# Two token mixers: how the decay sums and the adaLN rows are computed

## The chip, the cores and the metric

The kernel runs on one core of a Trainium2 chip. What counts is the device time of one execution in microseconds; less is better. A core has five engines with one instruction queue each: TensorE (PE in the profile, its weight loads PEld), VectorE (DVE), ScalarE (ACT), GpSimd (POOL) and SyncE (SP), which here issues the loads from memory. The engines meet only at semaphores.

## The reference

A trunk of two layers. Each layer is a feed-forward part, a token mixer and a second feed-forward part, each with its own modulation by a vector `c`. All sizes: 256 tokens, width 1024, float32 in and out.

```python
mod = (silu(c) @ w_ada[layer] + b_ada[layer]).reshape(b, 3, 3, 1, 1024)   # shift, scale, gate of each part
u = modulate(x, mod[:, 1, 0], mod[:, 1, 1])
m = hybrid_mixer(u, ...)                            # the token mixer
x = layer_norm(alpha * x + (1 + mod[:, 1, 2]) * m, ...)
u = modulate(x, mod[:, 2, 0], mod[:, 2, 1])         # second feed-forward part
# inside the mixer, scan over chunks with H = 8 heads:
a = dt * A
a_cs = cumsum(a)
decay = exp(where(causal, a_cs[l] - a_cs[s], -inf))
y_diag = einsum(C, B, decay, x * dt)
```

`mod` is nine rows of 1024 values per layer: one row vector times a 1024 x 1024 matrix for each. `decay` is, for each head, a 128 x 128 matrix for each of the two blocks of 128 tokens.

## The kernel before

The 256 tokens stand in two tiles of 128 (`t` = 0, 1). Every weight is streamed from memory once, as half tiles of 128 x 1024 float32 (512 KB, names `raw_...`). A pool has nine buffers for them (`NRAW`), and SyncE issues the loads in the order of use, up to nine ahead (`AHEAD`, `issue_loads`); a load into a buffer waits for the last reader of the tile that was in it. An ordinary weight is split: ScalarE casts it to a high part in fp32r (`h...`), VectorE subtracts to get the low part (`l...`). Each product of the large matrices is three fp32r matmuls (`mm3`): high by high, low by high, high by low.

The weights of `mod` are treated otherwise. Each of the nine rows of a layer (`ch` = 0 to 8) is a stream of eight half tiles `raw_(layer, ch, q)_h`. In `ada_step` VectorE multiplies a half tile by its 128 values of silu(c) and adds it to an accumulator `ada` of 128 x 1024. After the eighth, `ada_post` sums the 128 partitions by four float32 products with ones (`pr`, 32 equal rows for each 256 columns). A shift or scale row is copied by ScalarE (`adc`), turned into columns by TensorE (`pm`) and the bias is added. A gate row is split into `adg` (ScalarE's high part, VectorE's low part), spread over 128 partitions by fp32r products (`pg`) and VectorE writes `gate`; its bias is loaded into a row of the accumulator at the start.

Mixer 0 streams 16 such half tiles (its own gate, `ch` 5, then row 7, the scale of the part that follows); mixer 1 streams eight (its own gate). In both they stand between the input weights (`z`) and the output weights `w2`, `w3`, `w0`, `w1` of the mixer, two half tiles each.

Inside a mixer the order in which work is handed out is a string table `MIX` (`st` is one half tile of the stream, `am` `seg_pre`, `seg` the decay sums, `v` and `z` input products with names `ovx` and `ozx`, `y` `pdx`, `tf` `pyx`, which turns the result `yc` so that its features lie on the partitions, `p` the output projection `accx`). The order in which TensorE then runs its matmuls is fixed when the program is built: a scheduler takes from what the table handed out what its own estimate holds ready. Each engine runs its queue in that order.

The decay sums: `seg_pre` makes for each head `am`, the mask `gtm` scaled by that head's column of `a` (ScalarE, 128 x 128, eight for each `t`). `seg` multiplies each by the mask `tri` in one float32 product of 128 columns, four heads into one PSUM bank (`psex`), and ScalarE takes the exponential of the bank (`mtx`).

Elsewhere in the program one row of `mod` (at the very start, `adh`) is already computed on TensorE: `adh_step` multiplies raw half tiles by `cw` (silu(c) repeated in 32 columns), each product in its own group of 32 columns of the array (`tile_position`).

Of the kernel before, what the change touches and what calls it, by code (L numbers as in the profile page):

```python
# [11 lines left out]
F32 = mybir.dt.float32  # L12
# [54 lines left out]
def kernel(  # L67
# [87 lines left out]
    def split(src, hi, lo):  # L155
# [11 lines left out]
    gtm = cp.tile([P, P], F32, name="gtm")  # L167
    G.affine_select(out=gtm, in_=ones, compare_op=ALU.is_gt, fill=0.0, base=0,
                    pattern=[[-1, P]], channel_multiplier=1)
    neghalf = cp.tile([P, 16], F32, name="neghalf")  # L170
    G.memset(neghalf, -0.5)

# [41 lines left out]
    sel4r = cp.tile([P, 4], F32R, name="sel4r")  # L214
    V.tensor_copy(sel4r, sel4)

    ADA = ("ada", "adh")

    def hi_step():
        n = pos["hi"]  # L220
# [17 lines left out]
    def step(n=1):  # L238
        for _ in range(n):
            k = pos["lo"]  # L240
            if k >= 2 * len(items):
                return
            i, h = divmod(k, 2)
            kind, key, _ = items[i]
            issue_loads(k + 1)
            if kind in ADA:
                pos["hi"] = max(pos["hi"], k + 1)
                {"ada": ada_step, "adh": adh_step}[kind](key, raws.pop(k), h)
            else:
                if pos["hi"] <= k:  # L250
                    hi_step()
                ht, lt = tiles[kind, key][h]
                keep(V.tensor_tensor(lt, raws.pop(k), f(ht), op=ALU.subtract), "v")
            pos["lo"] += 1
            issue_loads(k + 1 + AHEAD)
# [53 lines left out]

    mods, gates, adas = {}, {}, {}  # L310

    def plan_ada(l, ch, q):
        plan("ada", (l, ch, q), w_ada[l, q * 256:(q + 1) * 256, ch * D:(ch + 1) * D])

    def plan_mod(l, s):
        return [(l, 3 * s + w, q) for w in range(2) for q in range(4)]
# [4 lines left out]
    def ada_step(key, raw, k):  # L321
        l, ch, q = key
        kt = 2 * q + k
        s, w = divmod(ch, 3)
        if kt == 0:
            adas[l, ch] = wtile([D], f"ada{l}_{ch}")
            if w == 2:
                G.memset(adas[l, ch], 0.0)
                nc.sync.dma_start(adas[l, ch][0:1, :], b_ada[l, ch * D:(ch + 1) * D].unsqueeze(0))
        acc = adas[l, ch]  # L330
        if kt == 0 and w < 2:
            keep(V.tensor_scalar(acc, raw, cT[:, 0:1], None, op0=ALU.mult), "v")
        else:
            keep(V.scalar_tensor_tensor(acc, raw, cT[:, kt:kt + 1], acc, op0=ALU.mult, op1=ALU.add), "v")
        if kt == KT - 1:
            late.append(lambda: ada_post(l, s, w, adas.pop((l, ch))))


    half_mods = {}
# [46 lines left out]
        else:  # L386
            V.scalar_tensor_tensor(md, pp, 1.0, bc, op0=ALU.add, op1=ALU.add)

    def ada_post(l, s, w, acc):

        ch = 3 * s + w
        pr = mps(f"pr{l}_{ch}")
        for j in range(4):
            PE.matmul(pr[32 * j:32 * j + 32, 0:256], lhsT=ones[:, 0:32], rhs=acc[:, j * 256:(j + 1) * 256],
                      start=True, stop=True, tile_position=(0, 32 * j))
        if w == 2:
            gr = wtile([D], f"gate{l}_{s}")
            gates[l, s] = gr
            half = 1.0 if s == 1 else 0.5
            cpy = wtile([2, 256], f"adg{l}_{ch}", F32R)  # L400
            split(pr[:, 0:256], cpy[:, 0], cpy[:, 1])
            for h in range(2):
                pp = mps(f"pg{l}_{s}_{h}")
                for i in range(2):
                    j = 2 * h + i
                    for e in range(2):
                        PE.matmul(pp[:, i * 256:(i + 1) * 256], lhsT=sel4r[:, j:j + 1].broadcast_to([P, P]),
                                  rhs=cpy[:, e], start=(e == 0), stop=(e == 1))
                V.tensor_scalar(gr[:, h * 512:(h + 1) * 512], pp, 1.0, half, op0=ALU.add, op1=ALU.mult)
            return  # L410
        cpy = wtile([256], f"adc{l}_{ch}")
        S.copy(cpy, pr[:, 0:256])
        pp = mps(f"pm{l}_{ch}")
        for k in range(2):
            PE.transpose(pp[:, k * P:(k + 1) * P], cpy[:, k * P:(k + 1) * P], ident)
        mod_cols(l, s, w, pp[:, 0:256].rearrange("p (k j r) -> p j k r", k=2, j=4)[:, :, :, 0])
# [478 lines left out]
    class Mixer:  # L895
# [14 lines left out]
        def plan_rest(self):  # L910
            for b in (2, 3, 0, 1):
                self.plan_cols(f"c{b}", X0 + b * BC)
            for n in "vz":
                for i in range(2):
                    self.plan_cols(f"{n}{i}", (V0 if n == "v" else Z0) + i * BC)
            for a in self.gate:
                plan_ada(*a)
            for a in self.ada:
                plan_ada(*a)
            for q in (2, 3, 0, 1):  # L920
                plan("rows", f"w{q}{self.nm}", self.wo2d[q * 256:(q + 1) * 256, :])

# [31 lines left out]
    def mixer(mx_, nxt):  # L954
# [251 lines left out]
        ssd = {}  # L1206

        def seg_pre(t):
            am = wtile([HEADS, P], f"am{nm}_{t}")
            for h in range(HEADS):  # L1210
                S.activation(am[:, h, :], gtm, AF.Identity, scale=aa[:, t, h:h + 1])
            ssd[t] = am

        def seg(t):
            am = ssd[t]
            mt = wtile([HEADS, P], f"mt{nm}_{t}")
            for g in range(2):
                ps = mps(f"pse{nm}_{t}{g}")
                for h in range(4):
                    PE.matmul(ps[:, h * P:(h + 1) * P], lhsT=am[:, 4 * g + h, :], rhs=tri, start=True, stop=True)  # L1220
                S.activation(mt[:, 4 * g:4 * g + 4, :], ps.rearrange("p (h k) -> p h k", h=4), AF.Exp)
            ssd[t] = mt

# [145 lines left out]
```

## Time and profile before

| | |
|---|---|
| median of 3 runs | 1079.92 us (1079.76 to 1083.99) |
| profiled execution | 1082.18 us, span 1080.3 us |
| TensorE busy | 1035.6 us (96%), mean granted clock 0.984 |
| VectorE busy | 835.1 us (77%) |
| ScalarE busy | 553.1 us (51%) |
| SyncE's loads | 257 MB, 239 GB/s over the span |

The span is what the profiler saw between the first and the last instruction; the 1.9 us that are left lie around it. The last input products (`ozx_1`) end at 322.5 us in mixer 0 and at 850.8 us in mixer 1. Busy times on TensorE overlap: a matmul starts before the one before it has left the array, so what one costs is read from start to start.

### The profile page before, as it was taken

How to read it: one execution, taken by the hardware profiler on the slowest of the kernel's cores; microseconds unless marked ns; L12 is line 12 of the kernel's file. 1: busy time of each engine (PE TensorE's matmuls, PEld its weight loads, DVE VectorE, ACT ScalarE, POOL GpSimd, SP SyncE). 2: the span in 40 equal slices, each digit the busy share in tenths (PEclk: the TensorE clock that was granted, in tenths of full speed). 3: DMA queues.
4: the chain of work that ended last, by engine and by line, in shares of the span. 5: the costliest groups of instructions: out<-in, count | busy, mean ns of one | idle time of the engine just before them, and what ended most of it. 6: DMA issues, size and time to landing. Idle time of an engine off the chain costs nothing.

```text
span 1080.3 us, 18994 instructions
## 1 busy us (share of the span) xinstructions
PE 1035.6 (96%) x7433; PEld 950.9 (88%) x7433; DVE 835.1 (77%) x1310; ACT 553.1 (51%) x946; POOL 53.0 (5%) x93
## 2 busy tenths in 40 slices
PE   4999999999997999999999999999999989999996
PEld 2799999989895899999988999998989979999995
DVE  5788688689988898769489768856999888756454
ACT  3475344476654664434466434546566567435241
POOL 1000000020010200000010000000100120000000
PEclk8999999999998999999999999999999999999999
DMA  9989888838368398789637889784664738776411
GB/s 343 311 301 383 292 291 313 295 114 270 100 202 281 120 307 306 293 323 328 237 117 259 302 317 362 277 288 126 174 212 141 230 101 304 247 241 214 161 40 39
DMA packets 162557, 258.24 MB, mean 239 GB/s; under 512 B 10806, under 2 KB 125982, under 8 KB 162468
## 3 DMA queue, kind: packets, MB, share of 16 engines
q1 hardware_dynamic: 162468, 257.04, 69.4%
q8 instruction: 58, 0.95, 0.3%
q14 instruction: 31, 0.25, 0.1%
HBM read 255.96 MB, written 1.05 MB: 238 GB/s over the span
## 4 chain that ended last, share of the span: by engine, by line
PE 77%; DVE 11%; ACT 6%; DMA 2%; issue 2%; POOL 1%; SPq 0%; DVEq 0%; POOLq 0%; ACTq 0%
PE ob L105 37%; PE acc L105 18%; PE oa L105 6%; PE oqkx L105 5%; PE accx L105 3%; PE ocx L105 2%; DVE xs L105 1%; PE ovx L105 1%; DVE ada L105 1%; DVE acc L105 1%; DVE cax L105 1%; PE pr L105 1%; ACT um L105 1%; ACT junk L105 1%; DVE lu L105 1%
## 5 line engine op out<-in xcount | busy, mean ns | idle before, releaser
L105 PE MATMUL ob<-uH,hg 128*128 128x256 f32 x576 | 163.1, 283 | 0.0
L105 PE MATMUL ob<-uL,hg 128*128 128x256 f32 x576 | 162.4, 282 | 0.0
L105 PE MATMUL ob<-uH,lg 128*128 128x256 f32 x576 | 161.8, 281 | 0.0
L105 PE MATMUL ob<-uH,hu 128*128 128x256 f32 x576 | 161.7, 281 | 0.0
L105 PE MATMUL ob<-uH,lu 128*128 128x256 f32 x576 | 161.7, 281 | 0.0
L105 PE MATMUL ob<-uL,hu 128*128 128x256 f32 x576 | 161.7, 281 | 0.0
L105 PE MATMUL acc<-ho,hH 128*128 128x512 f32 x352 | 137.5, 392 | 0.2 <-ACT hH L105 0.2
L105 PE MATMUL acc<-lo,hH 128*128 128x512 f32 x352 | 137.3, 390 | 0.0
L105 PE MATMUL acc<-ho,hL 128*128 128x512 f32 x352 | 137.2, 391 | 0.0
L105 ACT ACTIVATE sgb<-ob 128x256 f32<-128x256 f32 x72 | 27.6, 383 | 213.9 <-PE ob L105 213.3
L105 DVE TENSOR_TENSOR lo<-raw_o,ho 128x1024 fp32r<-128x1024 f32 x88 | 105.9, 1221 | 13.4 <-PE ob L105 6.5
L105 PEld LDWEIGHTS ob<-uH,hg 128*128 128x128 f32 x576 | 108.3, 188 | 7.8 <-issue 3.7
L105 PEld LDWEIGHTS ob<-uH,lg 128*128 128x128 f32 x576 | 110.2, 191 | 0.1
L105 PEld LDWEIGHTS ob<-uL,hg 128*128 128x128 f32 x576 | 108.2, 188 | 2.3
L105 PEld LDWEIGHTS ob<-uH,lu 128*128 128x128 f32 x576 | 110.2, 191 | 0.0
L105 DVE TENSOR_TENSOR lg<-raw_g,hg 128x1024 fp32r<-128x1024 f32 x84 | 100.6, 1221 | 11.5 <-ACT hg L105 6.1
L105 PEld LDWEIGHTS ob<-uH,hu 128*128 128x128 f32 x576 | 108.5, 188 | 0.0
L105 PEld LDWEIGHTS ob<-uL,hu 128*128 128x128 f32 x576 | 108.1, 188 | 0.0
L105 DVE TENSOR_TENSOR hfb<-ob,sgb 128x256 f32<-128x256 f32 x72 | 30.4, 422 | 94.4 <-ACT sgb L105 94.2
L105 DVE TENSOR_TENSOR lu<-raw_u,hu 128x1024 fp32r<-128x1024 f32 x84 | 100.6, 1220 | 3.5 <-ACT hu L105 1.9
L105 ACT CAST hg<-raw_g 128x1024 fp32r<-128x1024 f32 x84 | 86.3, 1050 | 32.0 <-PE acc L105 18.2
L105 ACT CAST ho<-raw_o 128x1024 fp32r<-128x1024 f32 x88 | 90.2, 1049 | 10.5 <-PE ob L105 9.0
(537 smaller groups left out, 2263.5 us busy)
## 6 DMA issues: line engine op xcount, KB each, us to landing
raw_o<-in_w_ffn_out_dram SPq DMA_DIRECT2D x88, 512.0 KB, 6.0
raw_g<-in_w_ffn_in_dram SPq DMA_DIRECT2D x84, 512.0 KB, 5.7
raw_u<-in_w_ffn_in_dram SPq DMA_DIRECT2D x84, 512.0 KB, 5.9
raw<-in_w_ffn_in_dram SPq DMA_DIRECT2D x8, 512.0 KB, 8.1
lg<-in_ln_g_dram SPq DMA_DIRECT2D x6, 512.0 KB, 6.2
lb<-in_ln_b_dram SPq DMA_DIRECT2D x6, 512.0 KB
raw_qk0x<-in_w_in_dram SPq DMA_DIRECT2D x4, 512.0 KB, 7.8
raw_qk1x<-in_w_in_dram SPq DMA_DIRECT2D x4, 512.0 KB
```

The source lines that it names most:

```text
L105: ins = emit(*args, **kwargs)
```

## The change

The `mod` rows of the two mixers no longer go through VectorE. Four raw half tiles are held; then TensorE multiplies them by `cw` in four narrow products that stand side by side in the array, once for each 512 columns, into one PSUM bank (`pa`), and ScalarE copies the bank to a row tile `adp`. Two such groups of four make a row; `ada_post` sums the partitions of both (eight products `pr` instead of four). The gate's bias is loaded to all partitions as 512 KB and added with `gate`. In `seg_pre` each head's column of `a` is split in a high and a low part and `tri` is scaled by both (16 activations for each `t`, not eight); in `seg` a bank is filled by two fp32r products of 512 columns with the mask `gtmr` as the weight. The table `MIX` is the same.

```diff
--- before.py
+++ after.py
@@ -167,6 +167,8 @@
     gtm = cp.tile([P, P], F32, name="gtm")
     G.affine_select(out=gtm, in_=ones, compare_op=ALU.is_gt, fill=0.0, base=0,
                     pattern=[[-1, P]], channel_multiplier=1)
+    gtmr = cp.tile([P, P], F32R, name="gtmr")
+    G.tensor_copy(gtmr, gtm)
     neghalf = cp.tile([P, 16], F32, name="neghalf")
     G.memset(neghalf, -0.5)
@@ -214,7 +216,7 @@
     sel4r = cp.tile([P, 4], F32R, name="sel4r")
     V.tensor_copy(sel4r, sel4)
-    ADA = ("ada", "adh")
+    ADA = ("ada", "adh", "adp")
     def hi_step():
         n = pos["hi"]
@@ -245,7 +247,7 @@
             issue_loads(k + 1)
             if kind in ADA:
                 pos["hi"] = max(pos["hi"], k + 1)
-                {"ada": ada_step, "adh": adh_step}[kind](key, raws.pop(k), h)
+                {"ada": ada_step, "adh": adh_step, "adp": adp_step}[kind](key, raws.pop(k), h)
             else:
                 if pos["hi"] <= k:
                     hi_step()
@@ -309,8 +311,8 @@
     mods, gates, adas = {}, {}, {}
-    def plan_ada(l, ch, q):
-        plan("ada", (l, ch, q), w_ada[l, q * 256:(q + 1) * 256, ch * D:(ch + 1) * D])
+    def plan_ada(l, ch, q, kind="ada"):
+        plan(kind, (l, ch, q), w_ada[l, q * 256:(q + 1) * 256, ch * D:(ch + 1) * D])
     def plan_mod(l, s):
         return [(l, 3 * s + w, q) for w in range(2) for q in range(4)]
@@ -333,7 +335,31 @@
         else:
             keep(V.scalar_tensor_tensor(acc, raw, cT[:, kt:kt + 1], acc, op0=ALU.mult, op1=ALU.add), "v")
         if kt == KT - 1:
-            late.append(lambda: ada_post(l, s, w, adas.pop((l, ch))))
+            late.append(lambda: ada_post(l, s, w, [(ones[:, 0:32], adas.pop((l, ch)))]))
+    def adp_step(key, raw, k):
+        l, ch, q = key
+        kt = 2 * q + k
+        s, w = divmod(ch, 3)
+        held, parts = adas.setdefault((l, ch), ([], []))
+        held.append(raw)
+        if len(held) < 4:
+            return
+        if kt == 3 and w == 2:
+            gates[l, s] = wtile([D], f"gate{l}_{s}")
+            nc.sync.dma_start(gates[l, s], b_ada[l, ch * D:(ch + 1) * D].partition_broadcast(P))
+        rows = wtile([D], f"adp{l}_{ch}_{kt}")
+        for h in range(2):
+            pa = mps(f"pa{l}_{ch}_{kt}{h}")
+            for i in range(4):
+                PE.matmul(pa[32 * i:32 * i + 32, :], lhsT=cw[:, kt - 3 + i, :], rhs=held[i][:, h * 512:(h + 1) * 512],
+                          start=True, stop=True, tile_position=(0, 32 * i))
+            S.copy(rows[:, h * 512:(h + 1) * 512], pa)
+        held.clear()
+        parts.append((sel1.broadcast_to([P, 32]), rows))
+        if kt == KT - 1:
+            late.append(lambda: ada_post(l, s, w, adas.pop((l, ch))[1], True))
     half_mods = {}
@@ -386,16 +412,18 @@
         else:
             V.scalar_tensor_tensor(md, pp, 1.0, bc, op0=ALU.add, op1=ALU.add)
-    def ada_post(l, s, w, acc):
+    def ada_post(l, s, w, parts, biased=False):
         ch = 3 * s + w
         pr = mps(f"pr{l}_{ch}")
-        for j in range(4):
-            PE.matmul(pr[32 * j:32 * j + 32, 0:256], lhsT=ones[:, 0:32], rhs=acc[:, j * 256:(j + 1) * 256],
-                      start=True, stop=True, tile_position=(0, 32 * j))
+        for n, (pick, acc) in enumerate(parts):
+            for j in range(4):
+                PE.matmul(pr[32 * j:32 * j + 32, 0:256], lhsT=pick, rhs=acc[:, j * 256:(j + 1) * 256],
+                          start=(n == 0), stop=(n == len(parts) - 1), tile_position=(0, 32 * j))
         if w == 2:
-            gr = wtile([D], f"gate{l}_{s}")
-            gates[l, s] = gr
+            if not biased:
+                gates[l, s] = wtile([D], f"gate{l}_{s}")
+            gr = gates[l, s]
             half = 1.0 if s == 1 else 0.5
             cpy = wtile([2, 256], f"adg{l}_{ch}", F32R)
             split(pr[:, 0:256], cpy[:, 0], cpy[:, 1])
@@ -406,7 +434,11 @@
                     for e in range(2):
                         PE.matmul(pp[:, i * 256:(i + 1) * 256], lhsT=sel4r[:, j:j + 1].broadcast_to([P, P]),
                                   rhs=cpy[:, e], start=(e == 0), stop=(e == 1))
-                V.tensor_scalar(gr[:, h * 512:(h + 1) * 512], pp, 1.0, half, op0=ALU.add, op1=ALU.mult)
+                hs = slice(h * 512, (h + 1) * 512)
+                if biased:
+                    V.scalar_tensor_tensor(gr[:, hs], pp, 1.0, gr[:, hs], op0=ALU.add, op1=ALU.add)
+                else:
+                    V.tensor_scalar(gr[:, hs], pp, 1.0, half, op0=ALU.add, op1=ALU.mult)
             return
         cpy = wtile([256], f"adc{l}_{ch}")
         S.copy(cpy, pr[:, 0:256])
@@ -913,10 +945,8 @@
             for n in "vz":
                 for i in range(2):
                     self.plan_cols(f"{n}{i}", (V0 if n == "v" else Z0) + i * BC)
-            for a in self.gate:
-                plan_ada(*a)
-            for a in self.ada:
-                plan_ada(*a)
+            for a in self.gate + self.ada:
+                plan_ada(*a, "adp")
             for q in (2, 3, 0, 1):
                 plan("rows", f"w{q}{self.nm}", self.wo2d[q * 256:(q + 1) * 256, :])
@@ -1206,18 +1236,21 @@
         ssd = {}
         def seg_pre(t):
-            am = wtile([HEADS, P], f"am{nm}_{t}")
+            ssd[t] = am = [wtile([HEADS, P], f"am{e}{nm}_{t}", F32R) for e in "hl"]
+            ah = sm.tile([P, HEADS], F32R, tag="ah", name=f"ah{nm}_{t}", bufs=2)
+            al = sm.tile([P, HEADS], F32, tag="al", name=f"al{nm}_{t}", bufs=2)
+            split(aa[:, t, :], ah, al)
             for h in range(HEADS):
-                S.activation(am[:, h, :], gtm, AF.Identity, scale=aa[:, t, h:h + 1])
-            ssd[t] = am
+                S.activation(am[0][:, h, :], tri, AF.Identity, scale=f(ah)[:, h:h + 1])
+                S.activation(am[1][:, h, :], tri, AF.Identity, scale=al[:, h:h + 1])
         def seg(t):
             am = ssd[t]
             mt = wtile([HEADS, P], f"mt{nm}_{t}")
             for g in range(2):
                 ps = mps(f"pse{nm}_{t}{g}")
-                for h in range(4):
-                    PE.matmul(ps[:, h * P:(h + 1) * P], lhsT=am[:, 4 * g + h, :], rhs=tri, start=True, stop=True)
+                for e in range(2):
+                    PE.matmul(ps, lhsT=gtmr, rhs=am[e][:, 4 * g:4 * g + 4, :], start=(e == 0), stop=(e == 1))
                 S.activation(mt[:, 4 * g:4 * g + 4, :], ps.rearrange("p (h k) -> p h k", h=4), AF.Exp)
             ssd[t] = mt
```

The order of issue is the same outside the two mixers. Three places inside mixer 0 are shown. The first is TensorE where the input products `ozx_1` end; before, the turn of `yc01`, the first output products and the eight products `pdx_1` follow.

```order
L105 MATMUL ozx_1_3731<-hz1x_1_3210,uL 128x256
L105 MATMUL pyx_01_3829<-ident,yc01x_3617 128x128 x4
L105 MATMUL accx_0_0_3916<-hw2x_0_3805,uH 128x512
L105 MATMUL pdx_1_3836<-xdx_2745,mtx_1_3520 128x64 x8
L105 MATMUL accx_0_0_3916<-lw2x_0_3806,uH 128x512
L105 MATMUL accx_0_1_3917<-hw2x_0_3805,uH 128x512
L105 MATMUL accx_0_1_3917<-lw2x_0_3806,uH 128x512
L105 MATMUL pr_5_3871<-ada_5_3324,ones 32x256 x4
L105 MATMUL accx_0_0_3916<-hw2x_0_3805,uL 128x512
L105 MATMUL accx_0_1_3917<-hw2x_0_3805,uL 128x512
```

Now, 16 narrow products of row 7 follow `ozx_1` (rows `pa_7_30`, `pa_7_31`, `pa_7_70` and `pa_7_71`; the last five are shown), and the rest comes behind them.

```order
L105 MATMUL pa_7_70_3845<-raw_(0, 7, 3)_1_3626,cw 32x512
L105 MATMUL pa_7_71_3851<-raw_(0, 7, 2)_0_3467,cw 32x512
L105 MATMUL pa_7_71_3851<-raw_(0, 7, 2)_1_3512,cw 32x512
L105 MATMUL pa_7_71_3851<-raw_(0, 7, 3)_0_3560,cw 32x512
L105 MATMUL pa_7_71_3851<-raw_(0, 7, 3)_1_3626,cw 32x512
L105 MATMUL pyx_01_3883<-ident,yc01x_3642 128x128 x4
L105 MATMUL pdx_1_3890<-xdx_2747,mtx_1_3551 128x64 x8
L105 MATMUL accx_0_0_3977<-hw2x_0_3859,uH 128x512
L105 MATMUL accx_0_0_3977<-lw2x_0_3860,uH 128x512
L105 MATMUL accx_0_1_3978<-hw2x_0_3859,uH 128x512
L105 MATMUL pr_5_3925<-adp_5_3_3454,sel_all 32x256 x4
L105 MATMUL pr_5_3925<-adp_5_7_3658,sel_all 32x256 x4
```

The four groups of narrow products have moved in between `ozx_1` and `pyx_01`, and the gate's sum `pr_5` has twice the products.

The second is SyncE: the loads of mixer 0's output weights, and the engine whose semaphore each waits for. Before, that is VectorE's, with `ada` or the low part of a weight as the last reader of the buffer (`DMAHW` is the semaphore of an earlier load).

```order
L203 DMA raw_w2x_0_3634<-in_w_out_dram 128x1024 [waits DMAHW6_49,DVE_49]
L203 DMA raw_w2x_1_3782<-in_w_out_dram 128x1024 [waits DMAHW7_49,DVE_49]
L203 DMA raw_w3x_0_3785<-in_w_out_dram 128x1024 [waits DMAHW0_49,DVE_49]
L203 DMA raw_w3x_1_3788<-in_w_out_dram 128x1024 [waits DMAHW6_49,DMAHW1_49,DVE_49]
L203 DMA raw_w0x_0_3791<-in_w_out_dram 128x1024 [waits DMAHW2_49,DVE_49]
L203 DMA raw_w0x_1_3794<-in_w_out_dram 128x1024 [waits DMAHW3_49,DMAHW7_49,DVE_49,Activation_49]
L203 DMA raw_w1x_0_3797<-in_w_out_dram 128x1024 [waits DMAHW4_49,DVE_49]
L203 DMA raw_w1x_1_3800<-in_w_out_dram 128x1024 [waits DMAHW5_49,DVE_49]
```

Now it is TensorE's semaphore:

```order
L205 DMA raw_w2x_0_3671<-in_w_out_dram 128x1024 [waits DMAHW6_49,PE_49]
L205 DMA raw_w2x_1_3817<-in_w_out_dram 128x1024 [waits DMAHW7_49,PE_49]
L205 DMA raw_w3x_0_3819<-in_w_out_dram 128x1024 [waits DMAHW0_49,PE_49]
L205 DMA raw_w3x_1_3821<-in_w_out_dram 128x1024 [waits DMAHW1_49,PE_49]
L205 DMA raw_w0x_0_3836<-in_w_out_dram 128x1024 [waits DMAHW2_49,PE_49]
L205 DMA raw_w0x_1_3838<-in_w_out_dram 128x1024 [waits DMAHW3_49,PE_49]
L205 DMA raw_w1x_0_3840<-in_w_out_dram 128x1024 [waits DMAHW4_49,PE_49]
L205 DMA raw_w1x_1_3842<-in_w_out_dram 128x1024 [waits DMAHW5_49,PE_49]
```

The buffers were last read by the narrow products: that of `w2x_0` by the second half of `pa_5_7`, those of `w2x_1` to `w0x_0` by `pa_7_31`, those of `w0x_1` to `w1x_1` by `pa_7_71`.

The third is VectorE before the gate of mixer 0 is written. Before:

```order
L105 SCALAR_TENSOR_TENSOR ada_7_3780<-raw_(0, 7, 3)_0_3534,cT,ada_7_3780 128x1024
L105 TENSOR_TENSOR uL<-pyx_01_3829,uH 128x512
L105 SCALAR_TENSOR_TENSOR ada_7_3780<-raw_(0, 7, 3)_1_3601,cT,ada_7_3780 128x1024
L105 TENSOR_TENSOR yv1x_3845<-pdx_1_3836,xkx_2746 128x512
L105 TENSOR_TENSOR lw0x_0_3848<-raw_w0x_0_3791,hw0x_0_3847 128x1024
L105 TENSOR_TENSOR lw0x_1_3854<-raw_w0x_1_3794,hw0x_1_3853 128x1024
L105 TENSOR_TENSOR lw1x_0_3860<-raw_w1x_0_3797,hw1x_0_3859 128x1024
L105 TENSOR_TENSOR lw1x_1_3866<-raw_w1x_1_3800,hw1x_1_3865 128x1024
L105 TENSOR_TENSOR adg_5_3877<-pr_5_3871,adg_5_3877 128x256
L105 SCALAR_TENSOR_TENSOR zt1x_3942<-zt1x_3942,ozx_1_3731 128x512
L105 TENSOR_SCALAR gate_1_3876<-pg_1_0_3880 128x512
```

Now:

```order
L105 TENSOR_TENSOR lw0x_0_3902<-raw_w0x_0_3836,hw0x_0_3901 128x1024
L105 TENSOR_SCALAR syx_1_4007<-syx_1_4007 128x2
L105 TENSOR_TENSOR lw0x_1_3908<-raw_w0x_1_3838,hw0x_1_3907 128x1024
L105 SCALAR_TENSOR_TENSOR yc10x_4013<-yv1x_3899,ryx_1_4011,snwx_2733 128x256 x2
L105 TENSOR_TENSOR lw1x_0_3914<-raw_w1x_0_3840,hw1x_0_3913 128x1024
L105 TENSOR_TENSOR lw1x_1_3920<-raw_w1x_1_3842,hw1x_1_3919 128x1024
L105 TENSOR_TENSOR adg_5_3934<-pr_5_3925,adg_5_3934 128x256
L105 SCALAR_TENSOR_TENSOR gate_1_3452<-pg_1_0_3937,gate_1_3452 128x512
L105 SCALAR_TENSOR_TENSOR gate_1_3452<-pg_1_1_3943,gate_1_3452 128x512
```

The `ada` operations are gone from between the low parts, and the gate's `adg` stands behind the low part of the last output weight, as it did.

## Rows read from the trace of the kernel before

**Rows 1.** Windows: busy us of PE, PEld, DVE, ACT, POOL; granted clock, DMA share, GB/s.
```profile
287.80:322.50 34.70, 34.44 (x291) 33.82 (x290) 31.30 (x52) 17.04 (x50) 2.62 (x2) 1.00 0.58 180
322.50:344.60 22.10, 15.44 (x80) 10.88 (x78) 18.73 (x26) 8.23 (x15) 2.15 (x2) 0.77 0.90 300
344.60:362.10 17.50, 17.29 (x76) 13.90 (x77) 14.79 (x28) 11.98 (x19) 2.60 (x7) 1.00 0.48 158
...
850.80:878.90 28.10, 27.68 (x145) 22.19 (x144) 22.98 (x40) 16.85 (x29) 2.84 (x7) 1.00 0.58 187
```

**Rows 2.** TensorE's waits from 322.5 to 344.6: us in total, times, longest.
```profile
PE pr L105 <- DVE uL L105: 3.0, 1, 3.0
PE pdx L105 <- DVE yc11x L105: 1.9, 1, 1.9
...
```

**Rows 3.** Chain of waits around mixer 0: start, us, what.
```profile
308.94 5.24 DMA raw_w2x<-in_w_out_dram
...
324.19 3.34 DMA raw_w1x<-in_w_out_dram
...
351.52 10.78 PE accx L105 x47
...
```

**Rows 4.** Narrow products early on, TensorE's timeline: start, us, operation, [idle before].
```profile
...
33.35 1.05 PE L105 MATMUL adh<-raw_(0, 1, 0)_1_228,cw 128*32 128x512 f32 x4
34.33 2.15 PE L105 MATMUL oa<-l,uH 128*128 128x256 f32 x16
36.41 0.62 PE L105 MATMUL adh<-raw_(0, 1, 1)_0_232,cw 128*32 128x512 f32 x2
...
37.41 0.74 PE L105 MATMUL oa<-h,uH 128*128 128x256 f32 x4
...
```

**Rows 5.** A group of decay sums in mixer 0, TensorE's timeline.
```profile
...
304.00 1.05 PE L105 MATMUL psex<-tri,amx 128*128 128x128 f32 x8
304.89 0.49 PE L105 MATMUL paTx<-ident,prx 128*128 128x128 f32 x3
```

**Rows 6.** TensorE's timeline into mixer 0's output projection.
```profile
...
322.49 0.60 PE L105 MATMUL pyx<-ident,yc01x 128*128 128x128 f32 x4
...
326.25 2.07 PE L105 MATMUL pdx<-xdx,mtx 128*128 128x64 f32 x16 [1.88 <-DVE yc11x L105]
...
335.16 0.63 PE L105 MATMUL accx<-lw2x,uH 128*128 128x512 f32 x1
335.59 0.63 PE L105 MATMUL accx<-hw2x,uL 128*128 128x512 f32 x1
...
341.93 0.64 PE L105 MATMUL pr<-ada,ones 128*32 128x256 f32 x8 [0.32 <-DVE gate L105]
...
344.61 0.50 PE L105 MATMUL accx<-hw0x,uH 128*128 128x512 f32 x1 [0.20 <-ACT uH L105]
...
```

**Rows 7.** VectorE's timeline in mixer 0.
```profile
...
290.54 1.27 DVE L105 SCALAR_TENSOR_TENSOR ada<-raw_(0, 5, 0)_0_2912,cT,ada 128x1024 f32<-128x1024 f32 x1
...
332.56 1.28 DVE L105 SCALAR_TENSOR_TENSOR ada<-raw_(0, 7, 3)_1_3601,cT,ada 128x1024 f32<-128x1024 f32 x1
...
336.62 2.36 DVE L105 TENSOR_TENSOR lw1x<-raw_w1x,hw1x 128x1024 fp32r<-128x1024 f32 x2
338.89 0.42 DVE L105 TENSOR_TENSOR adg<-pr,adg 128x256 fp32r<-128x256 f32 x1
...
```

**Rows 8.** ScalarE's copies of a bank of narrow products: min/median/max ns.
```profile
...
L105 ACT COPY adc<-adh x2: 586/586/587, 17.8 to 37.6; 128x512 f32<-128x512 f32 x2
...
```

**Rows 9.** ScalarE's timeline in mixer 0.
```profile
...
299.31 2.44 ACT L105 ACTIVATE amx<-gtm,aax 128x128 f32<-128x128 f32 x8
...
331.30 1.04 ACT L105 CAST hw1x<-raw_w1x 128x1024 fp32r<-128x1024 f32 x1 [2.60 <-DMA raw_w1x<-in_w_out_dram]
...
```

**Rows 10.** Windows of ten microseconds, columns as in Rows 1.
```profile
...
400.00:410.00 10.00, 10.00 (x76) 9.53 (x75) 9.89 (x10) 0.79 (x2) 0.00 (x0) 1.00 1.04 376
330.00:340.00 10.00, 7.29 (x27) 5.21 (x28) 9.91 (x11) 1.42 (x2) 0.00 (x0) 0.59 0.97 322
...
```

## The prediction

> **What bounds the kernel now.** I read the busy shares first, then windows over the two mixers, since the change touches nothing else, then TensorE's waits where the windows show it idle, and its timeline there. In mixer 0 TensorE is busy 34.44 of 34.70 us up to the end of the input products `ozx_1` at 322.49, with VectorE close behind (31.30) and ScalarE at half (17.04). Then come 22.1 us in which it is busy only 15.44, and at a mean granted clock of 0.77; then 17.29 of 17.50 [rows 1]. The same tail in mixer 1 takes 28.1 us with 27.68 busy [rows 1], against 22.1 + 17.5 = 39.6 in mixer 0. So the whole of mixer 1 and the head of mixer 0 are bound by TensorE itself, where VectorE's relief buys nothing, and some microseconds of stall lie in one stretch of mixer 0. The two waits that make most of it end in VectorE: 3.0 us for `uL` and 1.9 us for `yc11x` [rows 2]. The low parts end late there too: `lw1x` at 338.98, with the gate's `adg` right behind it at 338.89, and the second half of the output projection starts at 344.61 [rows 6, 7].
>
> **Removed.** 24 operations on VectorE, 16 in mixer 0 (the first and last in [rows 7]) and 8 in mixer 1, at 1.27 us, about 30 us. On TensorE 16 float32 decay products in each mixer, in four groups; a group takes 0.89 us from start to start [rows 5].
>
> **Added on TensorE.** A group of decay sums is now two products of 512 columns in fp32r. Such products run at 10.78 / 47 = 0.229 us each [rows 3], so 0.46 for a group, and each mixer saves 4 x (0.89 - 0.46) = 1.7 us.
>
> A group of four narrow products is in the trace once, early in the program: it starts at 36.41, the next work at 37.41, so 1.00 us [rows 4]. In that there are two passes over the columns, for float32. Two products alone took 0.98 us, from 33.35 to 34.33 [rows 4], so that a piece of a group costs as much as a whole one. Behind another group I take 0.86 us, twice the step of two passes (an estimate: less than the lone group's 1.00 by what its start and end add). The order puts the first product of mixer 0's gate by itself, then the other three with the next group, then two single groups: 1.00 + 1.86 + 2 x 1.00 = 4.86 us. Row 7 is four groups in one run: 1.00 + 3 x 0.86 = 3.58. Mixer 1 has the gate alone, 4.86 again. In `ada_post` a row has twice the `pr` products, and four of them last 0.64 us [rows 6]; 0.5 us more a row.
>
> The row in [rows 4] shows the lone group at 1.00 us. The Trainium skill's "TensorE: Matmul & The Clock Gate", Part 3, gives products side by side the time of one and about 4 ns for each further one; its "TensorEngine Tiling (Array Packing)", Key Properties, says that changing the tiling mode drains the engine. By the first alone the nine pieces that stand apart would cost about 0.86 like the others, and the sum would be about 1.2 us less; the trace's 1.00 goes with a drain at both ends.
>
> **Added elsewhere.** ScalarE: 32 more activations, eight of which take 2.44 us [rows 9], and twelve copies of 0.586 us [rows 8], on an engine that is half idle where they stand [rows 1]; I cost them at nothing, since the table hands out `am` ahead of `seg`. If that cover failed, the decay sums would wait for the 16 activations of a block, 4.9 us instead of 2.4: up to 2.4 us a mixer. The two gate biases are 512 KB, 1.4 us of the loads' full rate (376 GB/s [rows 10]), in a stretch with DMA at 0.58 [rows 1]. GpSimd's part is nothing.
>
> **Where the stall of mixer 0 goes.** Follow the new path. Up to the end of `ozx_1`: +4.86 - 1.7, and +0.4 because the last group of the gate needs a PSUM bank that the attention's `yc01x` must leave first (bounds 0 and 1). That is 322.49 + 3.6 = 326.1. The four groups of row 7 end at 329.7. What follows depends on loads. Before, the output weights' loads waited for VectorE's `ada`, and went out one by one from 308.94 to the last pair at 324.19 [rows 3]. Now `w2x_1` to `w0x_0` wait for the second group of row 7, 326.1 + 1.86 = 328.0, and the last three for its fourth. Seven half tiles then go out at once: 3.34 us for the first (that of `raw_w1x` [rows 3]) and six more at 1.39 us (376 GB/s) to 1.63 us (322 GB/s) [rows 10]. `w1x_1` lands between 339.7 and 341.1, say 340.4. Its cast takes 1.04 us [rows 9], its low part half of 2.36 [rows 7]: 342.7; 0.8 for another operation that is queued ahead on one of the two makes 343.5. There before it was 338.98. The gate's `adg` stands behind these two on ScalarE and VectorE, so `pg`, `gate`, then `pr_7`, `pm` and `pyx_00` stay behind the last output weight. Before, this tail took 344.61 - 338.89 = 5.72 us [rows 6, 7]; TensorE will be freer for `pg` (-0.9) and `pr_7` longer (+0.5), so 5.3. The second half of the output projection starts at 348.8, not 344.61: +4.2 us. VectorE is idle meanwhile. The stall is not removed but turned from a wait for VectorE into a wait for loads.
>
> In this stretch TensorE had half its clock before (1.2 of 2.4 GHz; 0.59 granted on the mean from 330 to 340 [rows 10]): steps of 0.43 us instead of 0.229 [rows 3, 6], after the two waits. TensorE will now be idle more often between 333 and 348, waiting for each half tile; if it is still at half clock when the last half of the projection starts, 24 products lose about 0.2 us each, 4 us at most, if not, nothing, or it gains the little that is hidden anyway. I take +1.0.
>
> **The sum.** Mixer 0: 4.2 + 1.0 = 5.2. The rest of it, 17.5 us, is bound by TensorE and unchanged. Mixer 1: its loads come out early enough (the output weights are cast while `ozx` runs), TensorE is full before and after, so its own time counts whole: 4.86 - 1.7 + 0.5 for `pr` + 0.4 for the bank = 4.1. Together +9.3 us on the profiled 1080.3 us of span; the execution's own 1082.18 is 2.3 us above the median of the runs, so I put the sum on the median: 1079.92 + 9.3 = 1089.2 us.
>
> **Bounds.** A narrow group below 1.00: one pass instead of two, 0.5 us, would take some 6 us off the 13.3; above, four one after the other at 0.86 each, 3.4 us. The loads: 1.39 or 1.63 us a tile, +-0.7. The clock: 0 to +3.5. The bank: 0 to 1 in each mixer. Without the two far ends this makes 1086 to 1093.
>
> **Rivals.**
> First, not slower: the stall goes. Mixer 0's tail is 39.6 - 28.1 = 11.5 us longer than mixer 1's [rows 1], of which the row 7 work (`pr`, `pm`) is about 1.0; 10.5 us can be won back, if the loads don't end late and the clock stays up. Against that stand 4.86 + 3.58 - 1.7 + 1.0 = 7.7 on TensorE; -2.8 in mixer 0, +3.6 in mixer 1, in sum +0.8: 1080.7. It decides if `w1x_1`'s low part is done before about 337, which would need the loads released ahead of row 7's groups. For it speaks that VectorE loses 30 us of work exactly where it is waited for; against it, that the buffers hang on TensorE now. Chance 0.19.
>
> Second, faster: narrow groups at half price (0.5 us) on top of the first rival: 1080.7 - 6.3 = 1074.4. Against it, the row with 1.00. Chance 0.06.
>
> Third, the change doesn't do what it says: groups with four different raw tiles don't run side by side. 13 pieces with 48 products at 0.86 are 41 us instead of 13.3: +28, 1117. The trace shows two raw tiles in one group at 1.00. Chance 0.03.
>
> Fourth, worse than forecast by the mechanism itself: half clock through the rest of mixer 0's projection and the slow load rate, +3.5 and +1.5: 1094 and more. Chance 0.10.
>
> The forecast has the remaining 0.62, with its own range of 1086 to 1093. The range from 1079.5 to 1095 takes in the greater part of the first rival and half of the fourth; left out are the second (0.06), the third (0.03), a quarter of the first (0.05) and half of the fourth (0.05), 0.19. What a measurement of this kernel can tell from no change is 0.5%, 5.4 us: below 1074.5 is faster, above 1085.3 slower. Slower takes the forecast, the third and the fourth, less 0.02 of the forecast that ends below 1085.3: 0.73; no change 0.21; faster 0.06.
>
> **What would show it.** In the profile after: a lone narrow group 1.00 us from start to start, four in a row 3.6; a group of decay sums 0.46; `ozx_1` in mixer 0 ending at 326 and its first-half output products waiting for `raw_w2x` and `raw_w3x` loads that were issued at about 328 in a burst; SyncE waiting for TensorE's `pa`; `lw1x` ending at 343 to 344; mixer 1's `ozx_1` 3.6 us later against its own start. It is wrong if the loads of `w1x` go out before 326, if TensorE waits less than 4 us between `ozx_1` and the second half of the projection, or if mixer 1 is not longer by 3 to 5 us.

## The result: 1.5% slower, beyond the forecast range

The changed kernel takes 1096.78 us (median of 4, 1095.59 to 1096.87), the kernel before 1079.84 (median of 4): a ratio of 1.0153 (95% interval 1.0139 to 1.0166), or +16.9 us. Forecast were +9.3 us and a range from 1079.5 to 1095. The direction was right, the size was not.

The two profiled executions differ by less, 1093.9 - 1080.3 = 13.6 us of span. The windows of the changed kernel that answer to [rows 1] (head and the two parts of mixer 0's tail, then the head and tail of mixer 1; the busy columns are TensorE, weight loads, VectorE, ScalarE, GpSimd, then the granted clock):

```profile
287.40:326.06 38.66, 38.30 (x298) 32.59 (x297) 18.99 (x44) 20.65 (x66) 2.69 (x3) 1.00 0.33 121
326.06:350.47 24.41, 18.30 (x128) 11.11 (x127) 14.79 (x20) 13.31 (x22) 1.67 (x1) 0.93 0.93 339
350.47:371.58 21.11, 17.20 (x77) 13.87 (x77) 13.41 (x25) 11.95 (x19) 2.14 (x6) 1.00 0.41 136
825.80:864.30 38.50, 38.14 (x297) 32.62 (x297) 24.55 (x49) 27.28 (x73) 2.69 (x3) 1.00 0.49 166
864.30:892.60 28.30, 28.06 (x154) 22.61 (x153) 22.83 (x40) 15.90 (x28) 2.85 (x7) 1.00 0.60 199
```

VectorE is indeed relieved in the head of mixer 0 (18.99 us for 31.30), and TensorE's time grows there by 38.66 - 34.70 = 4.0 us, as it was full. Mixer 0's tail is 24.4 + 21.1 = 45.5 us, where before it was 39.6: no stall was won back. Mixer 1 is 4.2 us longer from its `oqkx` to the end of `ozx_1` (98.4 for 94.2), and as long in its tail (28.3 for 28.1).

TensorE's waits from 326 to 372 us (total, times, longest) are new ones in the place of [rows 2]:

```profile
PE ptp L105 <- DVE xn L105: 3.9, 1, 3.9
PE pg L105 <- DVE adg L105: 2.8, 1, 2.8
PE pg L105 <- ACT adg L105: 1.8, 1, 1.8
PE pdx L105 <- ACT adp L105: 0.8, 1, 0.8
...
```

The waits for `adg` are those that were forecast behind the late output weights. The 0.8 us for `adp`, ScalarE's copy of a narrow group's bank, was costed at nothing. The largest wait, for `xn`, was not forecast: it stands behind the output projection, in the 17.5 us that I had called unchanged. TensorE's timeline shows the places (start, length, operation, what it waited for):

```profile
326.06 0.62 PE L105 MATMUL pa<-raw_(0, 7, 0)_0_3216,cw 128*32 128x512 f32 x1
...
329.76 0.66 PE L105 MATMUL pyx<-ident,yc01x 128*128 128x128 f32 x4
331.18 2.00 PE L105 MATMUL pdx<-xdx,mtx 128*128 128x64 f32 x16 [0.77 <-ACT adp L105]
...
341.82 0.39 PE L105 MATMUL pg<-adg,sel4r 128*128 128x256 f32 x1 [1.85 <-ACT adg L105]
345.00 1.86 PE L105 MATMUL pg<-adg,sel4r 128*128 128x256 f32 x7 [2.79 <-DVE adg L105]
...
350.47 0.50 PE L105 MATMUL accx<-hw0x,uH 128*128 128x512 f32 x1 [0.20 <-ACT uH L105]
...
371.58 0.82 PE L105 MATMUL ptp<-ident,xn 128*128 128x128 f32 x4 [3.91 <-DVE xn L105]
```

And VectorE's before `xn` (`uL` and `uH` are the low and high part of a turned block, `lg`, `lu` the low parts of the next part's first weights, `xs` and `accx` behind them the layer norm):

```profile
357.33 0.69 DVE L105 TENSOR_TENSOR uL<-pyx,uH 128x512 fp32r<-128x512 f32 x1 [5.60 <-ACT uH L105]
358.28 2.36 DVE L105 TENSOR_TENSOR lg<-raw_g,hg 128x1024 fp32r<-128x1024 f32 x2 [0.26 <-ACT hg L105]
360.56 1.22 DVE L105 TENSOR_TENSOR lu<-raw_u,hu 128x1024 fp32r<-128x1024 f32 x1
361.70 0.69 DVE L105 TENSOR_TENSOR accx<-accx,gate 128x512 f32<-128x512 f32 x1
...
370.89 1.00 DVE L105 TENSOR_SCALAR xn<-xs,nmqp,rmp 128x512 f32<-128x512 f32 x2 [0.70 <-POOL rmp L181]
```

VectorE sits idle for 5.6 us for the last turned block (`uL` of `pyx_10`). The low parts of the next part's first weights and then the layer norm of the first tokens are queued behind it. On ScalarE the casts `hg` of the same weights, whose loads went out at 331.7 and landed some 10 us later, stand behind `uH` of that turn; before, they stood ahead of it (before, then now):

```profile
344.94 2.00 ACT L105 CAST hg<-raw_g 128x1024 fp32r<-128x1024 f32 x2
...
351.56 0.58 ACT L105 CAST uH<-pyx 128x512 fp32r<-128x512 f32 x1 [1.68 <-PE pyx L105]
```

```profile
356.72 0.59 ACT L105 CAST uH<-pyx 128x512 fp32r<-128x512 f32 x1 [5.81 <-PE pyx L105]
357.20 2.00 ACT L105 CAST hg<-raw_g 128x1024 fp32r<-128x1024 f32 x2
```

The order of issue on VectorE shows the same. Before, `lg`, `lg`, `lu` and the layer norm's first operations stand ahead of that `uL`:

```
TENSOR_TENSOR uL<-pyx_11_3979,uH 128x512
TENSOR_TENSOR lg_0_0_4044<-raw_g_0_0_3803,hg_0_0_4043 128x1024
TENSOR_TENSOR lg_0_1_4050<-raw_g_0_1_3809,hg_0_1_4049 128x1024
TENSOR_TENSOR lu_0_0_4056<-raw_u_0_0_3815,hu_0_0_4055 128x1024
TENSOR_TENSOR accx_0_0_3916<-accx_0_0_3916,gate_1_3876 128x512
SCALAR_TENSOR_TENSOR xs,s1p_1_0_4067<-xs,accx_0_0_3916 128x512
TENSOR_TENSOR accx_0_1_3917<-accx_0_1_3917,gate_1_3876 128x512
TENSOR_TENSOR uL<-pyx_10_3986,uH 128x512
```

Now it is ahead of all of them, and TensorE has `pyx_10` behind 24 products of the second half, as before:

```
TENSOR_TENSOR uL<-pyx_11_4040,uH 128x512
TENSOR_TENSOR uL<-pyx_10_4047,uH 128x512
TENSOR_TENSOR lg_0_0_4105<-raw_g_0_0_3857,hg_0_0_4104 128x1024
```

A table of stages makes all runs comparable: from the first product of one name to the first of the next (projection half: the first product with `w0`; `ptp` is the first turn of the next part), in us. "Again" are second profiled executions, on another chip. In the forecast, 1.0 of the 4.2 us that the second half was to start later is the gate's first group, which stands in the first stage; the clock's 1.0 was put on the 24 products of the second half.

| stage | before | before again | changed | changed again | forecast of the change |
|---|---|---|---|---|---|
| mixer 0, `oqkx` to `ovx` | 59.7 | 59.5 | 60.8 | 60.8 | +1.0 |
| `ovx` to second projection half | 56.5 | 56.0 | 62.1 | 63.1 | +3.2 |
| second half to `ptp` | 17.5 | 17.5 | 21.1 | 21.1 | 0, and +1.0 for the clock |
| `ptp` to mixer 1's `oqkx` | 394.5 | 394.3 | 394.3 | 396.6 | 0 |
| mixer 1, `oqkx` to `ptp` | 122.5 | 121.8 | 126.7 | 126.4 | +4.1 |

### The profile page after: what moved, and what is told of

Same layout as the page of the kernel before. It is cut to its first block, busy times and chain, and to the rows that moved or that the text cites. A ratio compares the mean times of both kernels' runs of the same rounds, so it can differ in the third digit from the quotient of the medians.

```text
span 1093.9 us, 19154 instructions
## 1 busy us (share of the span) xinstructions
PE 1045.9 (96%) x7505; PEld 948.1 (87%) x7505; DVE 810.8 (74%) x1290; ACT 569.2 (52%) x994; POOL 50.5 (5%) x92
## 4 chain that ended last, share of the span: by engine, by line
PE 84%; DVE 7%; ACT 3%; DMA 2%; issue 1%; POOL 1%; SPq 0%; DVEq 0%; POOLq 0%; ACTq 0%
PE ob L105 37%; PE acc L105 22%; PE oa L105 7%; PE accx L105 3%; PE oqkx L105 2%; PE ocx L105 2%; PE ovx L105 2%; PE ozx L105 2%; PE pr L105 1%; PE pa L105 1%; DVE xs L105 1%; ACT um L105 1%; PE pg L105 1%; DMA xs<-in_x_dram 1%; PE ptp L105 1%
```

## The experiments

Theory A: the loss is TensorE's time for the narrow products, the loads behind them, and the queue order at the end of mixer 0. Thirteen runs follow, three of them of a kernel already run; ratios are to the kernel before on the same chip. The diffs are shortened.

**The two halves of the change.** The first keeps the new `seg_pre` and `seg` and puts all `mod` rows back on VectorE; the second does the reverse.

```diff
# e1, e8                                      # e2
-            for a in self.gate + self.ada:    -  new seg_pre, seg, gtmr
-                plan_ada(*a, "adp")           +  those of before
+  plan_ada(*a), as before
```

> Only the decay sums are changed (fp32r products of 512 columns, sums split in a high and a low part); all adaLN rows stay on VectorE. Theory A (the loss is TensorE time of the narrow products, loads that hang on TensorE, and a new queue order at the end of mixer 0; the decay sums alone are a gain): mixer 1 shorter by 1.5 to 2.0 us, mixer 0 by 0 to 2.0 because its tail waits for VectorE as before; 1076 to 1078.5 us. Theory B (the 32 more activations on ScalarE and the split delay the decay sums): 0 to +5 us, 1080 to 1085, with TensorE waiting for ScalarE before a psex product.

> Only the adaLN rows of the two mixers are changed (narrow products); decay sums as before. Theory A: the changed kernel's loss plus what the decay sums gave back, 2 x 1.7 to 2.0 us: 16.9 + 3.7 = +20 us, 1100 us, with the same 3 to 4 us wait of TensorE for the layer norm at the end of mixer 0. Theory B (decay sums cost): +12 to +16 us, 1092 to 1096.

The decay sums alone: 1090.34 us, ratio 1.0083 (1.0064 to 1.0102), slower by 10, where I expected a gain. Theory B's 0 to +5 is too small as well, and TensorE does not wait ahead of a `psex` product. The rows alone: 1101.87, 1.0193 (1.0178 to 1.0208), near theory A's 1100, with the same 3.9 us wait for `xn`; in mixer 1 they add 6.1 us. In the presence of the narrow products the decay sums give back 1101.87 - 1096.78 = 5.1 us by the medians, 4.3 by the ratios (3.2 against the changed kernel run again), 1.9 of it in mixer 1's profile. They are a gain there and a loss where they stand alone. A second profile of the decay sums alone was taken:

> The decay sums alone once more, for a second profiled execution: five of six executions took 1089 to 1093 us at a mean granted clock of 0.977 to 0.981, the profiled one 1085.2 at 0.985. Theory F (the waits are the same in all, and TensorE's clock stays at half for longer after them): the same waits in mixer 0 and 1, and stretches at half clock longer by about twice the difference in time, 8 to 12 us. Rival G (other waits): a stall that the first profile does not have.

1088.55 us. TensorE's waits in mixer 0 show a longer form of [rows 2], 6.2 for 3.0 (5.1 in the first profile):

```profile
PE pr L105 <- DVE uL L105: 6.2, 1, 6.2
PE pdx L105 <- DVE yc11x L105: 2.0, 1, 2.0
PE accx L105 <- ACT uH L105: 1.7, 2, 1.5
PE ozx L105 <- ACT vt1x L105: 0.7, 1, 0.7
```

In mixer 1 `accx` waits 2.0 us for `uH`, and its first half of the projection takes 12.5 us for 7.9. So neither theory as written: the waits themselves are there in both profiles of it. In the order, the second block's `psex` now stands behind 46 products of `ozx_0`, and `pox_0` and `pdx_0` behind 67 of `ozx`, where before they had none and 4 ahead of them. ScalarE ends the 16 activations of that block at 306.81 here, and the first of its `psex` starts at 307.40, so its own time would not have let them start much earlier either. My reading is that all that follows is late by this. To test that, the low part is taken from ScalarE:

```diff
-                S.activation(am[1][:, h, :], tri, AF.Identity, scale=al[:, h:h + 1])
+            G.tensor_tensor(am[1], tri.unsqueeze(1).broadcast_to([P, HEADS, P]),
+                            al.unsqueeze(2).broadcast_to([P, HEADS, P]), op=ALU.mult)
```

> The decay sums alone (adaLN rows on VectorE, as in the first run of the study), but the low part of the scaled masks is made by GpSimd in one operation for each t; ScalarE has 8 activations for each t as in the kernel before. Theory H (the decay sums alone lose 10 us because 16 activations for each t make the second block's sums late, and the scheduler's order puts 65 products of ozx ahead of pox_0 and pdx_0; the waits and the half clock follow from that): psex of the second block back to its place, the added waits in mixer 0 and 1 gone, 1076 to 1081 us. Rival I (what is lost comes with the products of 512 columns themselves): 1086 to 1091 us.

1081.66 us, ratio 1.0013 (1.0003 to 1.0023): 8.7 us come back by the medians, 7.6 by the ratios. Rival I is out: the products of 512 columns are still there. The second block's `psex` is back, behind 7 products, as theory H had it; but its range of 1076 to 1081 is just missed, and it doesn't beat the kernel before. Whether the loss was ScalarE's time or the order that the scheduler made of it is not separated, since this edit takes away both. Mixer 1 is 1.0 us shorter than in the first profile of the kernel before and 0.3 than in the second. In mixer 0 the wait for `uL` did not go, 5.9 us for 3.0; the tail there still waits for VectorE:

```profile
PE pr L105 <- DVE uL L105: 5.9, 1, 5.9
```

**The price of a narrow group.** In mixer 1 each group is run twice.

```diff
-            for i in range(4):
+            for i in list(range(4)) * (1 + l):
```

> As the changed kernel, but in mixer 1 the narrow products of each bank are run twice (the second overwrites the first): 16 more narrow products, four more groups, each directly behind its like. Theory A: 0.86 to 1.0 us each, ovx to pyx in mixer 1 longer by 3.4 to 4.0 us, nothing else moved. If a group's products didn't run side by side: 4 x 3.4 = 13.8 us.

In its one execution `ovx` to the output projection grew from 39.68 to 43.74 us: 4.06 for four groups, 1.0 each. A group of one bank and its second run stand in overlapping rows, two passes each; the first product of each of the four passes:

```profile
834.55 0.62 PE L105 MATMUL pa<-raw_(1, 5, 0)_1_9122,cw 128*32 128x512 f32 x1
...
835.00 0.59 PE L105 MATMUL pa<-raw_(1, 5, 0)_1_9122,cw 128*32 128x512 f32 x1
...
835.43 0.59 PE L105 MATMUL pa<-raw_(1, 5, 0)_1_9122,cw 128*32 128x512 f32 x1
...
835.86 0.59 PE L105 MATMUL pa<-raw_(1, 5, 0)_1_9122,cw 128*32 128x512 f32 x1
```

A pass takes 0.43 us, and products of different raw tiles start within 0.03 us of each other. Side by side, as said.

**Where row 7 stands.** First it stays on VectorE, then it is handed out earlier.

```diff
# e3: gates "adp", self.ada as before
# e6: row 7 earlier
-  av 1,z 1,st 1,up z1,up w2,st 1,
+  av 1,up w2,z 1,st 1,up z1,st 1,
```

> As the changed kernel, but row 7 (8 half tiles, mixer 0) stays on VectorE; the two gates are narrow products. Theory A: the four groups of 3.7 us go from behind ozx_1 and the output weights' loads go out earlier than 328; ozx_1 of mixer 0 still ends about 326, its tail is no longer than the 39.6 us of before: mixer 0 +2 to +5 us and mixer 1 +4, 1085 to 1089 us. Rival C (what costs is any narrow group, wherever it stands, at 16.9/13 = 1.3 us a piece): five pieces fewer by count of 14, 16.9 - 4 x 1.3 = +11.7, 1091.5 us.

> As the changed kernel, but the table hands out row 7 (up w2) ahead of z 1: its four narrow groups then stand between the products ozx_1, the last two after 21 of the 48, not behind them. Nothing is taken away or added. Theory A (the output weights' loads hang on these groups): loads of w2x_1 to w1x_1 go out at about 322 to 325, not 328 to 330; lw1x ends near 340, not 344.6; second half of the projection 4 us earlier: 1091 to 1093.5 us. Rival E (the price of the narrow groups on TensorE is all): no change, 1095.5 to 1097.

With row 7 on VectorE: 1090.73, ratio 1.0094 (1.0079 to 1.0109); from `ovx` to the second half 56.2 us, no longer than before, and 1.9 us of the wait for `xn` left. So row 7's groups and what hangs on them are 6 us. The time alone does not decide: it lies above theory A's 1085 to 1089 and near rival C's 1091.5. But C's 1.3 us a group does not fit the 1.0 just measured, and the stage that came back is the one that theory A names. Handed out early, the loads do go out earlier (`w1x` at 329.19, 7.3 us behind the last `pox`; 10.2 in the changed kernel) and `lw1x` ends 4.4 us earlier by the same measure. But the second half starts only 1.6 us earlier: now `adg` has the next part's first cast ahead of it on ScalarE. Measured 1099.26 (1.0171, 1.0153 to 1.0189), no faster than the changed kernel (1.0153 and, run again, 1.0163); neither theory held. Both mixers use the table, so `up w2` moves in mixer 1 too, which has no row 7: its second half to `ptp` grew by 1.1 us. The rest was not followed up.

**The wait for `xn`.** Two ways to undo the queue order.

```diff
# e4                                  # e5
-  tf 1 1,tf 1 0,p 1 1,p 1 0,pre      -  up w0,p 0 0,tf 1 1,tf 1 0,p 1 1,
+  tf 1 1,p 1 1,tf 1 0,p 1 0,pre      +  up w0,tf 1 1,tf 1 0,p 0 0,p 1 1,
```

> As the changed kernel, but the table hands out the last turn of the mixer (tf 1 0) behind the product p 1 1, not ahead of it; that puts the casts and low parts of the next part's first weights ahead of the last uH and uL on ScalarE and VectorE, where the kernel before has them. Theory A: the 3.9 us wait of TensorE for xn at the end of mixer 0 goes, the rest stays: -3 to -4 us against the changed kernel, 1093 us, mixer 1 unchanged. Rival D (the layer norm is late because the loads and with them the low parts are late): no change, 1096.5.

> As the changed kernel, but the table hands out tf 1 1 and tf 1 0 ahead of p 0 0: in mixer 0 TensorE turns yc10 behind 4 products of the output projection's second half, not behind 24. VectorE's and ScalarE's queues stay as they are, with the last uH and uL ahead of the next part's first weights and of the layer norm; these now find their input 4.6 us earlier. Theory A (the queues are held by uH and uL of that turn, 5.6 us of idle VectorE): the 3.9 us wait of TensorE for xn goes, -3 to -4 us, 1092.5 to 1093.5 us. Rival D (late loads hold the low parts and so the layer norm): no change, 1096.5 us.

The first was no test of it, although its time is the one of rival D: 1096.43 (1.0145, 1.0130 to 1.0159). TensorE now has `pyx_10` behind 48 products, and VectorE waits in the middle of the layer norm (2.8 us of the wait for `xn` are left):

```profile
357.83 0.70 DVE L105 TENSOR_TENSOR accx<-accx,gate 128x512 f32<-128x512 f32 x1
363.72 0.69 DVE L105 TENSOR_TENSOR uL<-pyx,uH 128x512 fp32r<-128x512 f32 x1 [5.19 <-ACT uH L105]
```

The second puts `pyx_10` behind 4 products, and leaves VectorE's order alone. 1093.72 (1.0124, 1.0111 to 1.0138), 3.1 us less; second half to `ptp` is 17.0 us, and the wait for `xn` is gone:

```profile
PE pg L105 <- DVE adg L105: 2.8, 1, 2.8
PE pg L105 <- ACT adg L105: 1.9, 1, 1.9
PE pdx L105 <- ACT adp L105: 0.8, 1, 0.8
PE pm L105 <- ACT adc L105: 0.5, 1, 0.5
```

That is theory A. In the profile this stage is 4.1 us shorter than in the changed kernel's first, and the one ahead of it 1.0 us longer. Combinations:

> The two edits together, row 7 ahead of z 1 and both turns ahead of p 0 0. Theory A: both gains, 7 us against the changed kernel, 1089 to 1091; what is left against the kernel before is TensorE's added products, 2 x 4.2 us, and no stall. If this is under 1083, the added products cost less than I read.

> The changed kernel with both repairs: tf 1 1 and tf 1 0 ahead of p 0 0, and the low part of the scaled masks on GpSimd. Theory H: in the changed kernel TensorE is full where the decay sums stand, so ScalarE's load costs little there: 0 to -2 us against 1093.7 of the turns alone. Theory A: what is left is TensorE's added products in two mixers, 8 to 9 us, plus the wait for the output weights' loads, so not under 1089.

1096.25 (1.0141, 1.0127 to 1.0155), a miss: against the turns alone, mixer 0 gains 2.5 us up to the second half and loses 2.4 behind it, and mixer 1 is 2.2 us longer. And 1092.72 (1.0119, 1.0103 to 1.0134), where GpSimd's part is worth 1.0 us by the medians, less than the intervals can tell from nothing. No version that beats the kernel before was found.

**Medians against profiles.** Both kernels once more, on one chip:

> The changed kernel itself, for a second profiled execution and on one chip with the next. The medians differ by 16.9 us, the two first traces by 13.6. Theory J (TensorE's clock: the first trace of the kernel before had more half clock than most of its executions, and that of the changed kernel less): 1095.5 to 1098 us; a span of 1094 to 1096, the stages of mixer 0 as in the first trace within 0.5 us, and any further difference where the granted clock differs. Rival K (another stall outside the two mixers): a stage outside them longer by over 1 us at the same granted clock.

> The kernel before, for a second profiled execution. Theory J: 1078.5 to 1081 us, shorter than its first trace (1082.2), by less half clock in mixer 0 from 325 to 345 us (0.74 granted there in the first) or at the start; the same waits.

1098.29 (1.0163, 1.0149 to 1.0178) and 1080.45. The second profiles differ by 1097.4 - 1078.6 = 18.8 us. Against its first profile the changed kernel is longer by 1.0 us in the gate of mixer 0 and 2.2 in the next part (table). Behind the new waits the granted clock is lower (column behind the busy times); first profile, then second, and under each TensorE's waits for `xn` from there to mixer 1:

```profile
345.00:355.00 10.00, 9.30 (x53) 6.96 (x54) 2.84 (x5) 1.45 (x3) 0.00 (x0) 0.85 0.90 331
375.00:380.00 5.00, 5.00 (x30) 5.00 (x30) 4.85 (x13) 3.10 (x6) 1.88 (x2) 0.63 0.00 0
...
PE ptp L105 <- DVE xn L105: 3.9, 1, 3.9
```

```profile
345.00:355.00 10.00, 8.78 (x46) 6.47 (x47) 3.36 (x7) 1.48 (x3) 0.00 (x0) 0.68 0.96 354
375.00:380.00 5.00, 3.61 (x17) 3.54 (x17) 4.96 (x15) 4.48 (x10) 0.59 (x1) 0.50 0.00 0
...
PE ptp L105 <- DVE xn L105: 4.9, 2, 3.9
```

The other stages agree within 0.5 us. So theory J in the main: how long TensorE stays at 1.2 GHz behind the new waits differs between executions, and the 1.0 us and 1.5 of the 2.2 lie there. It is not the whole: the other 0.7 lies behind 571 us, where the second profile has a second wait for `xn`, of 1.0 us, that the first lacks and that both profiles of the kernel before have. The time and the span, 1098.29 and 1097.4, are also above the ranges put on theory J.

## Why the prediction was wrong, step by step

- **TensorE's added products: right, but for their edges.** Lone groups took 1.0 us as in [rows 4], four in a row 3.70 (forecast 3.58), a group of decay sums 0.46 to 0.54 (0.46), the wait for the bank 0.36 (0.4). Up to the end of `ozx_1` both mixers grew by more than the forecast 3.6 us, mixer 0 by 4.4 and mixer 1 by 4.2 in the first profile. The product ahead of a narrow group has 0.21 us and the one behind it 0.22 from start to start, not 0.12: 0.2 us for each of four interruptions, which the sum did not have. Mixer 1 as a whole grew by 4.2 and 4.6 us, forecast 4.1; that it fits so well is in part luck, as its second half to `ptp` became 0.5 us shorter.
- **The loads: right in mechanism, short in size.** They went out from 327.99 (forecast 328.0), `lw1x` ended at 344.6 (343.5), and from there to the second half it was 5.9 us (5.3): it began at 350.5 (348.8). From `ozx_1` to there it was 24.4 us in this profile and one other, and 25.4 in the second profile and in three of the experiments with the same order there, where the forecast had 22.7: short by 1.7 to 2.7 us. One thing that was to show it did not come: no output product of the first half waited for a load, the waits are those for `adg`.
- **"The rest of it, 17.5 us, is bound by TensorE and unchanged": this step failed.** It was 21.1 us. Behind the gate the order on VectorE and ScalarE changed, and a turn that TensorE runs late now holds the layer norm up. That is 3.6 us, of which the experiment with both turns first gave 3.1 back, to 1093.72, inside the forecast range. I had read the order of issue up to the gate and no further; the two listings above were there to be compared. Why the scheduler moved the operation is not shown; in its order `yc10` has come ahead of the gate. None of the three signs of being wrong appeared (the loads of `w1x` at 330.46, 6.1 us of waits between `ozx_1` and the second half, mixer 1 longer by 4.2): all of them look at places ahead of this step or away from it.
- **The clock: +1.0 forecast** for the second half's products. The granted clock was 1.00 there, and it cost nothing. It cost in other places, behind the new waits, by up to 2.5 us more in one execution than in another. Of the 3.3 us between 13.6 in the first profiles and 16.9 in the medians, 1.2 are the changed kernel's, whose profiled run was its shortest (1095.59); most of the rest is that the profiled run of the kernel before was 2.3 us above its median.
- **ScalarE's work at nothing: nearly right in the changed kernel only,** where TensorE is full at the place of the decay sums (about 1 us with GpSimd in their place, and 0.8 us of wait for a copy to `adp`). Alone, the activations cost 8.7 us by the medians, more than the 2.4 us a mixer that the prediction gave as the most.
- **The rivals.** "The stall goes" was wrong: VectorE's relief is real, but its queue waits for loads and then for a turn. The fourth rival had the right time, 1094 and more, by luck: it named half clock through the rest of the projection, which ran at 1.00 in the first profile, and not the queue. The third counts 13 pieces where the prediction's own split makes 14 (5, 4 and 5); it decides nothing.

## What to carry to other kernels

Here the work that VectorE no longer did was worth nothing, because the buffers that it had freed were now freed by TensorE, the engine that is the bound. Where a scheduler fixes the order, compare the order of every engine to the end of the stage, not only where the changed operations stand: a strict queue with one operation moved ahead cost 3 to 4 us here, as much as four added groups of products. Name a sign of being wrong for every stage, the ones called unchanged too. And price an edit of two parts by each part alone before adding: the decay sums gave -3 to -5 us together with the other part, +10 alone.

## What was not expected of the hardware

Executions of one program differ by 2.5 us behind the same waits, as the clock after a wait stays at its lower level for longer or shorter (0.85 or 0.68 granted from 345 to 355 us). Two profiles of such a pair can then differ by less than the medians do, 13.6 us against 16.9: the one run was the shortest of its kernel, the other lay 2.3 us above its median.
